# A two-layer hybrid decoder: the rotary table takes a buffer of the norms, and the last norm is cut differently between ScalarE, VectorE and GpSimd

## The chip, the cores and the metric

The kernel runs on one core of a Trainium2 chip. The metric is the device time of one execution in microseconds (us). A core has five engines: TensorE (PE in the profile, with its weight loads as PEld), VectorE (DVE), ScalarE (ACT), GpSimd (POOL) and SyncE (SP). Each works through its own list of instructions in order and waits on semaphores; all weights come in by DMAs that SP issues.

## The reference

One inference step of two decoder layers on 512 prompt tokens and 32 sample tokens (8 sequences of 4), width 1024, all float32. Cut to what matters here:

```python
def rms_norm(x, g):
    return x * lax.rsqrt(jnp.mean(x * x, axis=-1, keepdims=True) + NORM_EPS) * g

def partial_rope(x, pos):          # 16 of each head's 64 channels are rotated
    ang = pos[:, None] * inv[None, :]
    cos, sin = jnp.cos(ang), jnp.sin(ang)
    return jnp.concatenate([x1 * cos - x2 * sin, x2 * cos + x1 * sin, rest], -1)

def decoder_layer(x, start, st, prm):
    h = rms_norm(x, prm['g_mix_pre'])
    p_rw, p_s5, p_gdn, p_swa = split_cols(h @ prm['w_in'], PROJ_SPLITS)
    # RWKV-7 | S5 state space | gated DeltaNet | sliding-window attention (rotary on q and k)
    mix = jnp.concatenate([o_rw, o_s5, o_gdn, o_swa], -1) @ prm['w_out']
    x = x + rms_norm(mix, prm['g_mix_post'])
    h = rms_norm(x, prm['g_mlp_pre'])
    f = jnp.square(jax.nn.relu(h @ prm['w_up'])) @ prm['w_down']
    return x + rms_norm(f, prm['g_mlp_post'])
```

Outputs are the final x of all tokens and the updated states of the four mixers.

## The kernel before

The 544 tokens are columns and are worked on in two halves of 256 and 288 columns. Channels lie on the 128 partitions, eight tiles of 128 to the width. Activations of a half live in tiles named `acc` (128 x 8 x 288), the residual input is fetched back from DRAM as `xs`, `r` or `f`.

Every large product is made in three terms to keep float32 accuracy. A block of weights of 128 x 512 is loaded by SP (`wraw`, 256 KB, L1681, five buffers); ScalarE rounds it (`whi`, L232, three buffers); VectorE subtracts (`wlo`, L236, three buffers); TensorE then adds up hi x rh, hi x rl and lo x rh, twelve matmuls of 256 or 288 columns per block (L220), where rh and rl are the two parts of the activations (`h`, or `f` in the second half of the MLP). So each block needs one instruction of ScalarE, one of VectorE and one DMA, and a buffer of each of the three kinds comes free only when its readers are through.

A tile scheduler sets the order on each engine. It runs the program against its own model of time, with priorities for groups of work: mixers, norms, evacuations and weight loads. Code of one half is woven into the matrix products of the other in that way, so a changed buffer can move instructions far from the changed line. Buffers come from classes with a size and a count: `g2` (2304 bytes, 5 buffers) serves the mixers, `d2` (2304 bytes, 2 buffers) serves `prenorm`, `r2` and `r4` (5 buffers each) the mixers and the last norms. A tile of a class with no free buffer waits until the oldest one's last reader is done.

The order of the stages, each by layer and half: first projection, mixers of the first half beside the projection of the second, output product, MLP of one half beside the mixers of the other, and so on; the last stage is the second layer's MLP on the second half, with nothing left to weave in but the first half's final norm.

What the change and the prediction touch:

- `sw_begin` (L1085 to L1094) opens the sliding-window attention of a half. It takes a tile `rope` (cosines and sines, 128 x 2 x 288, so 256 to 288 KB), loads it with a DMA on SP (L1089) that is ordered after the last instruction of the gated DeltaNet before it, and `sw_evac` multiplies with it, once on GpSimd and once on VectorE for each of three tiles, when the projection of that half comes to the attention's columns. There are four such loads.
- `prenorm` (a few lines below `rms`) normalises a half ahead of a product. For each pair of tiles VectorE multiplies into a temporary of class `d2`, ScalarE scales two `h` tiles and VectorE makes the low parts, two instructions of the form SCALAR_TENSOR_TENSOR.
- `rms` and `rsqrt` (L1569 to L1582): two matmuls with a constant give the mean of squares, `preload_act_table_set` has ScalarE load a table (L1578, ACT_TABLE_LOAD) after the second matmul is placed, then come Ln and Exp on ScalarE. This happens 16 times in a run.
- `residual` (L1650 to L1672) computes x + norm. In the final one (`final`), it goes by four pairs of tiles, q = 0, 2, 4, 6: VectorE multiplies the pair by the norm, then adds the residual input; for q = 2 the addition is GpSimd's. SP writes each pair out (L1663). VectorE's order in the trace is four multiplies, then three additions.
- The final residual runs twice: for the first half inside the second half's MLP, for the second half as the end of the program.

Of the kernel before, what the change touches and what calls it, by code (L numbers as in the profile page):

```python
# [11 lines left out]
AF = mybir.ActivationFunctionType  # L12
ALU = mybir.AluOpType
# [6 lines left out]
HA = 288  # L20
# [119 lines left out]
class K:  # L140
# [944 lines left out]

    def sw_begin(self, l, half):
        n = HALVES[half][1]
        rope = self.w([128, 2, HA], "g2")[:, :, :n]
        d = self.nc.sync.dma_start(out=rope, in_=self.i["rope"][half, :, :, :n])  # L1089
        self.after(d, self.last_gd)  # L1090
        r = dict(n=n, half=half, x=self.place("sx", [128, 3, n]), v=self.place("sv", [128, n]), rope=rope)
        if half:
            r["prev"] = self.swprev
        return r  # L1094
# [471 lines left out]
        else:  # L1566
            self.last_sq = sq

    def rms(self, sums, sq):  # L1569

        n = sums.shape[1]
        mp = self.ps([128, n], "mn")
        self.mm(mp, self.mean.to_broadcast([128, 128]), sums, True, False)
        return self.rsqrt(sums, mp, self.mm(mp, self.mean.to_broadcast([128, 128]), sq, False, True))

    def rsqrt(self, out, mean, dep):

        t = self.nc.scalar.preload_act_table_set("natural_log_exp_and_others")  # L1578
        self.after(t, dep.ins)
        self.after(self.act(out, mean, AF.Ln, bias=self.eps), t.ins)  # L1580
        self.last_exp = self.act(out, out, AF.Exp, scale=-0.5)
        return out  # L1582

# [65 lines left out]
    def residual(self, half, src, sums, sq, cls, final=False):  # L1649


        c0, n = HALVES[half]
        xt = self.fetch(half, cls)
        rs = self.rms(sums, sq)
        step = 2 if final else 4
        new = None if final else self.row(half, "sums")
        mp = None
        for q in range(0, 8, step):
            a, xq = src[:, q:q + step], xt[q // 4][:, q % 4:q % 4 + step]
            self.tt(a, a, rs.unsqueeze(1).to_broadcast([128, step, n]))  # L1660
            self.tt(a, a, xq, ALU.add, eng=self.nc.gpsimd if final and q == 2 else None)
            if final:
                self.nc.sync.dma_start(out=self.o["yT"][:, q:q + step, c0:c0 + n], in_=a)  # L1663
            else:
                self.act(xq, a, AF.Square)
                mp = self.ps([128, n], "mn") if mp is None else mp
                for k in range(4):
                    m = self.mm(mp, self.mean.to_broadcast([128, 128]), xq[:, k], q + k == 0, q + k == 7)
        if final:
            return  # L1670
        self.x[half] = self.t([128, 8, n], f"x{half}", pool="dram", bufs=2)
        self.nc.gpsimd.dma_start(out=self.x[half], in_=src)  # L1672
        return self.rsqrt(new, mp, m)
# [387 lines left out]
```

## Time and profile before

| | |
|---|---|
| time, median of 3 runs | 1626.77 us (1626.5 to 1631.62) |
| profiled execution, its own time | 1630.86 us |
| its span, first to last instruction | 1629.1 us |
| PE busy in the span | 95% |
| PEld, DVE, ACT, POOL busy | 89%, 73%, 59%, 20% |
| mean granted clock of TensorE | 0.984 |
| DMA traffic | 267.38 MB, mean 164 GB/s |

The span and the rows below belong to the one profiled execution; it is 4.1 us above the median, inside what the three runs spread over. A name such as `wlo` stands for all buffers of that name; the line L236 is a helper that records every two-operand instruction, so what tells instructions apart there is what they read and write. A row that stands for several instructions gives the time from the first's start to the last's end.

### The profile page before, as it was taken

To read this page: it belongs to the slowest core of one execution; us is meant where nothing else is said; L and a number is where in the kernel's file an instruction comes from. 1 tells how busy PE (TensorE), PEld (TensorE's weight loads), DVE (VectorE), ACT (ScalarE), POOL (GpSimd) and SP (SyncE) were. 2 spreads that over 40 slices of the span, in tenths; PEclk is the share of its full clock that TensorE was granted. 3 is DMA by queue.
4 is the path that set the end of the run, shared out by engine and by line. 5 is a ranking of instruction groups with operands and counts; after the bars stand their busy time and mean duration, and the time that the engine had idled before them with its cause. 6 is when DMAs were issued, how large, how long until landed. Compare 5 with 4: busy or idle time off the path is not lost. (4 is left out here: it accounts for less than half of the span.)

```text
span 1629.1 us, 38773 instructions
## 1 busy us (share of the span) xinstructions
PE 1555.1 (95%) x14528; PEld 1453.4 (89%) x14528; DVE 1195.3 (73%) x2843; ACT 961.8 (59%) x2086; POOL 318.0 (20%) x618
## 2 busy tenths in 40 slices
PE   7989989899999999899999999999999999999996
PEld 7978978689889999888989999989888889999996
DVE  6898786976876867787595567879679755856665
ACT  6766648643455567765454467886444556755544
POOL 4751251000310428100020002620013001200001
PEclk9999999999999999999999999999999999999998
DMA  7645444443566565535365555535436655655552
GB/s 232 200 114 136 143 134 148 109 130 114 173 211 201 171 204 204 182 112 139 105 217 173 167 161 197 180 109 151 138 121 208 205 193 185 210 189 166 163 170 101
DMA packets 203112, 267.38 MB, mean 164 GB/s; under 512 B 81114, under 2 KB 95772, under 8 KB 202508
## 3 DMA queue, kind: packets, MB, share of 16 engines
q1 hardware_dynamic: 199180, 249.94, 48.9%
q0 software_dynamic: 3744, 14.96, 2.5%
q8 instruction: 114, 1.87, 0.5%
q14 instruction: 74, 0.61, 0.1%
HBM read 237.95 MB, written 28.58 MB: 164 GB/s over the span
## 5 line engine op out<-in xcount | busy, mean ns | idle before, releaser
L232 ACT CAST whi<-wraw 128x512 fp32r<-128x512 f32 x752 | 462.6, 619 | 419.2 <-PE ps L220 264.7
L236 DVE TENSOR_TENSOR wlo<-wraw,whi 128x512 fp32r<-128x512 f32 x752 | 534.9, 716 | 209.2 <-ACT whi L232 188.0
L220 PE MATMUL ps<-h,whi 128*128 128x288 f32 (+1 forms) x3264 | 519.5, 297 | 8.4 <-ACT h L228 4.4
L220 PEld LDWEIGHTS ps<-h,whi 128*128 128x128 f32 x3264 | 451.3, 191 | 25.8 <-ACT h L228 6.0
L220 PE MATMUL ps<-f,whi 128*128 128x288 f32 (+1 forms) x2752 | 421.9, 292 | 5.9 <-ACT whi L232 5.8
L220 PEld LDWEIGHTS ps<-f,whi 128*128 128x128 f32 x2752 | 372.0, 189 | 17.1 <-ACT whi L232 7.4
L220 PE MATMUL ps<-h,wlo 128*128 128x288 f32 (+1 forms) x1632 | 285.9, 295 | 5.4 <-DVE wlo L236 5.1
L220 PEld LDWEIGHTS ps<-h,wlo 128*128 128x128 f32 x1632 | 235.8, 191 | 12.3 <-DVE wlo L236 7.8
L220 PE MATMUL ps<-f,wlo 128*128 128x288 f32 (+1 forms) x1376 | 235.8, 292 | 1.7 <-DVE wlo L236 1.7
L220 PEld LDWEIGHTS ps<-f,wlo 128*128 128x128 f32 x1376 | 195.9, 189 | 5.3 <-DVE wlo L236 2.9
L236 POOL TENSOR_TENSOR sums<-sums,d 128x288 f32<-128x288 f32 (+1 forms) x54 | 51.2, 948 | 519.0 <-ACT d L228 517.7
L220 PE MATMUL ps<-r,r 64*64 64x64 f32 (+7 forms) x1184 | 67.8, 236 | 12.7 <-POOL r L236 3.8
L236 DVE TENSOR_TENSOR acc<-acc,ps 128x256 f32<-128x256 f32 (+1 forms) x96 | 41.7, 435 | 49.8 <-PE ps L220 49.7
L220 PEld LDWEIGHTS ps<-r,r 64*64 64x64 f32 (+4 forms) x1184 | 55.9, 140 | 23.2 <-issue 5.9
L232 ACT CAST f<-d 128x288 fp32r<-128x288 f32 (+1 forms) x128 | 53.3, 417 | 35.3 <-DVE d L236 35.3
L228 ACT ACTIVATE d<-ps 128x288 f32<-128x288 f32 (+1 forms) x152 | 59.8, 393 | 8.1 <-PE ps L220 6.1
L236 DVE TENSOR_TENSOR f<-d,f 128x288 fp32r<-128x288 f32 (+1 forms) x128 | 56.7, 443 | 7.4 <-ACT f L232 7.4
L236 DVE TENSOR_TENSOR d<-d 128x288 f32<-128x288 f32 (+1 forms) x128 | 56.7, 443 | 0.0
L228 ACT ACT_TABLE_LOAD x43 | 55.2, 1283 | 0.8
L220 PEld LDWEIGHTS ps<-t,t 64*64 64x64 f32 x1024 | 32.5, 135 | 4.7 <-issue 1.1
L220 PE MATMUL ps<-t,t 64*64 64x64 f32 x1024 | 36.3, 220 | 0.3 <-DMA t<-diag 0.2
L232 ACT COPY r<-ps 64x128 f32<-64x128 f32 (+2 forms) x56 | 20.4, 369 | 26.4 <-PE ps L625 11.6
(404 smaller groups left out, 1851.6 us busy)
## 6 DMA issues: line engine op xcount, KB each, us to landing
wraw<-in_w_up SPq DMA_DIRECT2D x256, 256.0 KB, 2.8
wraw<-in_w_down SPq DMA_DIRECT2D x256, 256.0 KB, 2.9
wraw<-in_w_in SPq DMA_DIRECT2D x176, 256.0 KB, 3.0
wraw<-in_w_out SPq DMA_DIRECT2D x64, 256.0 KB, 3.2
t<-diag SPq DMA_DIRECT2D x32, 128.0 KB, 3.2
x<-acc POOLq DMA_DIRECT2D x3, 1152.0 KB, 6.8
x<-acc POOLq DMA_DIRECT2D x3, 1024.0 KB, 6.4
xs<-mix SPq DMA_DIRECT2D x8, 288.0 KB, 2.9
```

Source lines behind the costliest of these rows:

```text
L220: return self.nc.tensor.matmul(out=out, lhsT=lhsT, rhs=rhs, start=start, stop=stop)
L228: return self.nc.scalar.activation(out=out, in_=in_, func=func, scale=scale, bias=bias, **kw)
L232: return self.nc.scalar.copy(out, in_)
L236: return (eng or self.nc.vector).tensor_tensor(out=out, in0=a, in1=b, op=op)
```

## The change

Three edits. The rotary table's tile is taken from `d2`, the two buffers of `prenorm`, instead of `g2`, the five of the mixers. `rms` and `rsqrt` get a flag, and the final residual of the second half asks for no ACT_TABLE_LOAD ahead of its Ln. In both final residuals, the pair q = 2 is multiplied on GpSimd as well as added there.

```diff
     def sw_begin(self, l, half):
         n = HALVES[half][1]
-        rope = self.w([128, 2, HA], "g2")[:, :, :n]
+        rope = self.w([128, 2, HA], "d2")[:, :, :n]
         d = self.nc.sync.dma_start(out=rope, in_=self.i["rope"][half, :, :, :n])
         self.after(d, self.last_gd)
...
-    def rsqrt(self, out, mean, dep):
-
-        t = self.nc.scalar.preload_act_table_set("natural_log_exp_and_others")
-        self.after(t, dep.ins)
-        self.after(self.act(out, mean, AF.Ln, bias=self.eps), t.ins)
+    def rsqrt(self, out, mean, dep, load=True):
+
+        ln = lambda: self.act(out, mean, AF.Ln, bias=self.eps)
+        if load:
+            t = self.nc.scalar.preload_act_table_set("natural_log_exp_and_others")
+            self.after(t, dep.ins)
+            self.after(ln(), t.ins)
+        else:
+            ln()
         self.last_exp = self.act(out, out, AF.Exp, scale=-0.5)
...
-        rs = self.rms(sums, sq)
+
+        rs = self.rms(sums, sq, not (final and half))
...
             a, xq = src[:, q:q + step], xt[q // 4][:, q % 4:q % 4 + step]
-            self.tt(a, a, rs.unsqueeze(1).to_broadcast([128, step, n]))
-            self.tt(a, a, xq, ALU.add, eng=self.nc.gpsimd if final and q == 2 else None)
+            eng = self.nc.gpsimd if final and q == 2 else None
+            self.tt(a, a, rs.unsqueeze(1).to_broadcast([128, step, n]), eng=eng)
+            self.tt(a, a, xq, ALU.add, eng=eng)
```

How the lists of instructions move, with the numbers of the buffers as the scheduler gave them. On SP, the rotary load of the second layer's first half stands 83 places later, between the weight blocks that were issued at 619.91 and 621.94 us in the trace of before, and waits there for a `d2` buffer; the second layer's other one stands three weight blocks later. The two of the first layer keep their places.

On DVE, the `prenorm` ahead of the first layer's MLP on the second half, which starts at 648.84 us in the trace of before: `d_2144` to `d_2147` are the four products in `d2` buffers, `h_2143` the low parts made from them, `xs_9094` work of the second layer's RWKV mixer.

```order
 L236 TENSOR_TENSOR wlo_9421<-wraw_9419,whi_9420 128x512
 L245 SCALAR_TENSOR_TENSOR h_2143_11270<-d_2144_11271,pf_73,h_2142_11269 128x288
+L236 TENSOR_TENSOR wlo_9452<-wraw_9450,whi_9451 128x512
+L236 TENSOR_TENSOR d_2145_11277<-acc_8396,sums_8788 128x576
+L245 SCALAR_TENSOR_TENSOR xs_9094<-e_1787_9394,pf_75,xs_9094 128x256
+L236 TENSOR_TENSOR wlo_9470<-wraw_9468,whi_9469 128x512
 L245 SCALAR_TENSOR_TENSOR h_2143_11270<-d_2145_11277,pf_73,h_2142_11269 128x288 x2
-L236 TENSOR_TENSOR wlo_9452<-wraw_9450,whi_9451 128x512
+L236 TENSOR_TENSOR wlo_9497<-wraw_9495,whi_9496 128x512
 L236 TENSOR_TENSOR d_2146_11283<-acc_8396,sums_8788 128x576
-L245 SCALAR_TENSOR_TENSOR xs_9094<-e_1787_9394,pf_75,xs_9094 128x256
-L236 TENSOR_TENSOR d_2147_11289<-acc_8396,sums_8788 128x576
```

In the order before, the multiply of `d_2145` stood right behind that of `d_2144`, ahead of these rows. It now follows the readers of `d_2144`; that of `d_2146` follows the readers of `d_2145`, and that of `d_2147` stands further on.

On PE, the products of that MLP (`ps_12065`, `ps_12107`, `ps_12149`, units of `w_up`) around the first S5 product (`ps_11078`), whose operand `r_2101` GpSimd makes; in the trace of before this is the stretch from 833 to 843 us.

```order
-L220 MATMUL ps_12107<-h_2142_11269,whi_12109 128x288 x4
+L220 MATMUL ps_12107<-h_2142_11269,whi_12109 128x288
+L220 MATMUL ps_12065<-h_2142_11269,wlo_12086 128x288 x4
+L220 MATMUL ps_12107<-h_2142_11269,whi_12109 128x288 x3
 L220 MATMUL ps_12107<-h_2143_11270,whi_12109 128x288 x4
+L220 MATMUL ps_12107<-h_2142_11269,wlo_12110 128x288 x4
+L220 MATMUL ps_12107<-h_2142_11269,whi_12127 128x288 x4
 L220 MATMUL ps_11078<-r_2101_11054,r_2106_11071 64x64 x2
 L220 MATMUL ps_11107<-r_2101_11054,r_2106_11071 64x64 x2
-L220 MATMUL ps_12065<-h_2142_11269,wlo_12086 128x288 x4
-L220 MATMUL ps_12149<-h_2142_11269,whi_12151 128x288 x4
-L220 MATMUL ps_12149<-h_2143_11270,whi_12151 128x288 x4
```

Twelve more matmuls of the MLP (`wlo_12086`, `wlo_12110`, `whi_12127`) now stand ahead of the S5 product, whose matmuls keep their own order.

On DVE, the final residual of the first half, from 1417.45 us in the trace of before: `acc_17066` is that half, `sums_17067` its norm, `r_3820` and `r_3821` the residual input; `f`, `d` and `wlo` belong to the second half's MLP.

```order
-L236 TENSOR_TENSOR acc_17066<-acc_17066,sums_17067 128x2x256 x4
+L236 TENSOR_TENSOR acc_17066<-acc_17066,sums_17067 128x2x256 x3
 L236 TENSOR_TENSOR wlo_20220<-wraw_20218,whi_20219 128x512
 L236 TENSOR_TENSOR acc_17066<-acc_17066,r_3820_20111 128x2x256
 L236 TENSOR_TENSOR f_3811_20068<-d_3819_20106,f_3810_20067 128x288
 L236 TENSOR_TENSOR d_3830_20170<-d_3830_20170 128x288
-L236 TENSOR_TENSOR acc_17066<-acc_17066,r_3821_20112 128x2x256
+L236 TENSOR_TENSOR acc_17066<-acc_17066,r_3821_20112 128x2x256 x2
 L236 TENSOR_TENSOR wlo_20238<-wraw_20236,whi_20237 128x512
-L236 TENSOR_TENSOR acc_17066<-acc_17066,r_3821_20112 128x2x256
```

One multiply is gone from the run of four ahead of `wlo_20220`, and two additions instead of one stand ahead of `wlo_20238`; on GpSimd a multiply stands ahead of the addition, and on SP the four writes of this half stand in a row instead of between weight blocks.

In the last residual there are now three multiplies and three additions on DVE, a multiply and an addition on POOL, and on ACT Ln right behind its work for the mean. Of SP's four writes there, GpSimd's pair was first before and is second now, behind the pair q = 0.

## Rows read from the trace of the kernel before

**Rows 1.** the page, part 1: engine, busy us, share of the span, instructions

```profile
PE 1555.1 (95%) x14528; PEld 1453.4 (89%) x14528; DVE 1195.3 (73%) x2843; ACT 961.8 (59%) x2086; POOL 318.0 (20%) x618
```

**Rows 2.** last MLP: us, busy us of PE, PEld, DVE, ACT, POOL, clock

```profile
1410.00:1616.00 206.00, 205.75 (x1543) 204.85 (x1542) 127.32 (x227) 111.16 (x219) 7.59 (x8) 1.00 0.51 165
```

**Rows 3.** what PE waited for: total us, times, longest us

```profile
PE ps L220 <- DVE wlo L236: 6.8, 12, 1.7
```

**Rows 4.** timeline of the tail: start, us, engine, line, operation, [idle before]

```profile
1616.56 0.75 PE L220 MATMUL ps<-e,mean 128*128 128x288 f32 x2 [0.53 <-ACT e L228]
1617.10 1.28 ACT L1578 ACT_TABLE_LOAD   x1
1618.39 0.50 ACT L228 ACTIVATE sums<-ps,eps 128x288 f32<-128x288 f32 x1
...
1619.40 3.96 DVE L236 TENSOR_TENSOR acc<-acc,sums 128x576 f32<-128x576 f32 x4 [3.36 <-ACT sums L228]
1620.90 1.85 POOL L236 TENSOR_TENSOR acc<-acc,xs 128x576 f32<-128x576 f32 x1 [6.55 <-DVE acc L236]
...
1623.29 2.08 DVE L236 TENSOR_TENSOR acc<-acc,xs 128x576 f32<-128x576 f32 x3
```

**Rows 5.** timeline, a norm between layers, PE and ACT

```profile
627.07 0.65 PE L220 MATMUL ps<-e,mean 128*128 128x288 f32 x2
...
627.82 0.50 ACT L228 ACTIVATE sums<-ps,eps 128x288 f32<-128x288 f32 x1 [0.24 <-POOL s5v L242]
```

**Rows 6.** timeline, final residual of the first half, inside the last MLP

```profile
1417.45 3.59 DVE L236 TENSOR_TENSOR acc<-acc,sums 128x512 f32<-128x512 f32 x4
...
1418.82 1.67 POOL L236 TENSOR_TENSOR acc<-acc,r 128x512 f32<-128x512 f32 x1 [5.91 <-DVE acc L236]
...
1420.96 0.68 DVE L236 TENSOR_TENSOR wlo<-wraw,whi 128x512 fp32r<-128x512 f32 x1
...
1422.08 0.70 PE L220 MATMUL ps<-h,wlo 128*128 128x288 f32 x4
...
1423.51 0.68 DVE L236 TENSOR_TENSOR wlo<-wraw,whi 128x512 fp32r<-128x512 f32 x1
...
1424.75 0.69 PE L220 MATMUL ps<-h,wlo 128*128 128x288 f32 x4
```

**Rows 7.** timeline around 621 us, DVE and SP

```profile
620.42 0.87 DVE L245 SCALAR_TENSOR_TENSOR f<-d,pf,f 128x256 fp32r<-128x256 f32 x2
...
621.94 0.93 SPq L1681 DMA_DIRECT2D wraw<-in_w_in  x2
```

**Rows 8.** DMA, 619 to 632 us: GB/s in 40 slices; issues, KB, landing

```profile
GB/s 214 44 0 0 0 38 221 397 170 6 0 13 145 347 303 189 258 171 100 136 182 234 248 298 362 379 390 393 395 405 401 457 377 381 382 389 398 391 384 328
...
wraw<-in_w_in SPq DMA_DIRECT2D x8, 256.0 KB, 7.3
```

**Rows 9.** timeline, PE after those loads

```profile
632.93 1.22 PE L220 MATMUL ps<-f,whi 128*128 128x256 f32 x8 [0.27 <-ACT whi L232]
634.60 1.21 PE L220 MATMUL ps<-f,whi 128*128 128x256 f32 x8 [0.46 <-ACT whi L232]
```

**Rows 10.** timeline, low parts of the moved norm, and their first reader

```profile
658.96 1.80 DVE L245 SCALAR_TENSOR_TENSOR h<-d,pf,h 128x288 fp32r<-128x288 f32 x4
...
722.03 0.83 PE L220 MATMUL ps<-h,whi 128*128 128x288 f32 x5
```

**Rows 11.** timeline, PE's larger gaps from 648 to 840 us

```profile
657.22 0.50 PE L220 MATMUL ps<-f,whi 128*128 128x256 f32 x2 [2.90 <-ACT whi L232]
...
663.99 1.21 PE L220 MATMUL ps<-f,whi 128*128 128x256 f32 x8 [0.85 <-ACT whi L232]
...
702.99 0.70 PE L220 MATMUL ps<-e,cst 128*128 128x256 f32 x2 [1.11 <-ACT e L232]
...
708.48 1.16 PE L220 MATMUL ps<-r,r 64*128 64x128 f32 x16 [0.82 <-DVE r L236]
...
837.18 0.45 PE L220 MATMUL ps<-r,r 64*64 64x64 f32 x8 [2.08 <-POOL r L236]
```

More of the change, by code (lines that the diff above doesn't have):

```diff
@@ L1567, in square_sum, with rms @@
             self.last_sq = sq
-    def rms(self, sums, sq):
+    def rms(self, sums, sq, load=True):
         n = sums.shape[1]
@@ L1573, in rms @@
         self.mm(mp, self.mean.to_broadcast([128, 128]), sums, True, False)
-        return self.rsqrt(sums, mp, self.mm(mp, self.mean.to_broadcast([128, 128]), sq, False, True))
-    def rsqrt(self, out, mean, dep):
-        t = self.nc.scalar.preload_act_table_set("natural_log_exp_and_others")
-        self.after(t, dep.ins)
-        self.after(self.act(out, mean, AF.Ln, bias=self.eps), t.ins)
+        return self.rsqrt(sums, mp, self.mm(mp, self.mean.to_broadcast([128, 128]), sq, False, True), load)
+    def rsqrt(self, out, mean, dep, load=True):
[6 more added lines that the diff above has]
+            ln()
         self.last_exp = self.act(out, out, AF.Exp, scale=-0.5)
```

## The prediction

> **What bounds the kernel now.** I read the page's busy shares first: TensorE is busy for 1555.1 us of the span [rows 1], so a change moves the time in two places only, where TensorE waits and where it has ended. Then the busy time by stretches: in the last MLP TensorE is busy for 205.75 of 206 us, and VectorE for 127.32 [rows 2], so VectorE's work counts there only if a `wlo` comes late. TensorE's list of waits holds such cases, 12 of them with 6.8 us together and 1.7 us at the longest [rows 3]. Last I read the timeline of the tail, where nothing hides anything [rows 4].
>
> **The last table load.** The two matmuls of the mean end at 1616.56 + 0.75 = 1617.31, ACT_TABLE_LOAD runs from 1617.10 to 1618.38 and Ln starts at 1618.39 [rows 4]. Without the load Ln waits for TensorE alone. The row nearest to that is the norm at 627, where ScalarE had loaded earlier: the matmuls end at 627.72 and Ln starts at 627.82, 0.10 later [rows 5]. So Ln starts at 1617.41 and the tail gains 0.98 us. Bounds: 0 if ScalarE finds something else to wait for, 1.08 if Ln follows TensorE at once. The load shows no idle time ahead of it, and Ln follows 0.01 us behind it [rows 4]. The Trainium skill (ScalarE: Activation LUTs, What ACT_TABLE_LOAD costs) puts a switch to another set at about 2.66 us, 1.283 of load and 1.380 of drain. The load agrees with the row's 1.28; a drain would bring the gain to some 2.4 us, an estimate from that page, but the rows leave it no room on either side, and I give it no chance.
>
> **GpSimd's multiply in the tail.** Three VectorE additions take 2.08 us, 0.69 each, with GpSimd idle; the four multiplies take 3.96 where 4 x 0.69 = 2.77 would do, with GpSimd's 1.85 us inside their time [rows 4]. So GpSimd's one operation takes 1.19 us out of VectorE's, and the two do not run side by side. Before: 3.96 + 2.08, less the overlap of 0.07, is 5.97 from 1619.40 to 1625.37. After: six VectorE operations, 6 x 0.69 = 4.16, and two of GpSimd at 1.19, 2.38, together 6.54. That is 0.57 longer. Bounds: if the second GpSimd operation costs VectorE nothing, one multiply less, -0.69; if both shut VectorE out for their full 1.85, 4.16 + 3.70 = 7.86, +1.9. I take +0.57, since it uses the only rate that the rows show for this pair of shapes. SP's last write stays that of a VectorE pair, behind the last addition, so what follows it stays. Tail: -0.98 + 0.57 = **-0.4** us, between -1.8 and +1.9.
>
> **The same multiply in the first half's residual.** It lies inside the last MLP. Four multiplies of 512 columns took 3.59 us [rows 6]; at 0.69 x 512/576 = 0.62 each they would take 2.47, so GpSimd's 1.67 us cost VectorE 1.12 here. After the change: 3 x 0.62 + 2 x 1.12 = 4.10, which is 0.51 longer. Behind that stands a `wlo` that ended at 1421.64 and that TensorE took at 1422.08: 0.44 us of slack, so it comes 0.07 late. The next one ended at 1424.19 and was taken at 1424.75, 0.56 of slack [rows 6]; it has the 0.51 and one more addition of 0.62 ahead of it, and comes 0.57 late. TensorE loses the larger of the two, and the loss stays, since this stretch has no idle time in which to make it up: **+0.6** us. Bounds: 0 if GpSimd's multiply slips behind the first `wlo`; if both operations block in full, 1.86 + 3.34 = 5.20, which is 1.61 longer, and the second `wlo` comes 1.61 + 0.62 - 0.56 = 1.7 late. SP issues four writes in a row there before its next weight block; that block is for later, and its other buffers cover it.
>
> **The rotary load.** The loads of the first layer and the second layer's last one stay in or near their places; I cost them at nothing, and lose nothing if wrong, as their readers come tens of us later. The second layer's first one moves into a crowd. Its wait for a `d2` buffer costs nothing: the buffer's last readers end at 620.42 + 0.87 = 621.29, and the weight load behind it was issued at 621.94 [rows 7], so SP is not held and neither are the weights queued behind. But 256 KB more then lie ahead of the loads that take 7.3 us to land, in slices that move some 390 GB/s [rows 8]; 0.262 MB at that rate is 0.67 us. TensorE then already waits 0.27 and 0.46 us for the `whi` made from them [rows 9], so there is no cover left and I count it in full: **+0.7** us, between 0 (the casts wait for a free buffer) and 1.0 (several blocks late).
>
> **The buffer that is gone.** With the table in one of two `d2` buffers, the four multiplies of the norm for the first layer's second MLP go one at a time. The low parts ended at 658.96 + 1.80 = 660.76, and TensorE first reads the result at 722.03 [rows 10]; even 10 us later nobody waits for it. The other norm of this kind, for the second layer's first half, is cheap for the same reason. What it does cost or give is order: from there to 840 us the scheduler weaves VectorE's and TensorE's lists anew. Five of TensorE's waits there sum to 7.76 us [rows 11]. In the new order twelve more matmuls stand ahead of the S5 product that waited 2.08 us for GpSimd; at 1.21/8 = 0.15 us each [rows 9] they cover up to 1.8. Two stand ahead of the product that waited 1.11 (0.5 covered, with their loads), and eleven ahead of the one that waited 0.82 (all of it). Of the 2.90 us at 657.22 about 1.0 goes, as TensorE takes the blocks that are there first; but ScalarE then comes later to the block at 663.99, whose wait grows by about 0.75. Together -1.8 - 0.5 - 0.8 - 1.0 + 0.75 = -3.35. A new order also brings waits at places that had none, and no trace of before shows them, while I looked for gains only where a wait stood. I keep half: **-1.7** us, between -3.4 and +3.4, the same on the other side.
>
> **Sum.** -0.4 + 0.6 + 0.7 - 1.7 = -0.8 us. Against the profiled execution's own 1630.86 this gives 1630.1. That execution lies 4.1 us above the median, with a span shorter by 1.8; the terms are differences, so on the median they give 1626.77 - 0.8 = **1626.0**. A difference of 0.3%, 4.9 us, is about what a measurement of this kernel can tell from none.
>
> **The rivals.** (a) The new order closes the waits without opening others: all of the 3.35, then as much again from the mixers beyond 1000 us, whose lists on TensorE also move, with the tail and the residual at their good ends (-0.4 and 0) and the load hidden: -7, so 1619.8. For it: 7.76 us of waits lie there. Against it: waits are there because operands are late, and matmuls put ahead only help if their own weights are ready. (b) GpSimd and VectorE shut one another out in full, and the load is late: tail +0.9 (-0.98 + 1.9), residual +1.7, load +1.0, order 0, together +3.6, so 1630.4. For it: GpSimd's 1.85 us cost VectorE 1.19 already. The Trainium skill (GPSIMD Engine Reference, 4.1 Engine selection) gives element-wise work with two inputs to VectorE, GpSimd being about 2 times slower; that speaks against this edit, and the rows, 1.85 against 0.69 us with both at work, show a wider ratio. (c) Slower: the norm that now goes through one `d2` buffer stalls VectorE. Each of its last three multiplies stands behind ScalarE's reading of the pair before it, and `wlo` blocks stand behind the multiply in VectorE's list. If ScalarE is held by a late weight block, TensorE waits for those `wlo` too; with one wait like the 2.90 of [rows 11] at two of the three, and the load's 0.7, +6.5 and 1633.3. It decides once ScalarE's copies come later than VectorE has other work, some 0.7 us by one instruction. (d) The change does not do what it says: Ln is held until 1618.39 by another wait, so the 0.98 is lost: +0.2, 1627.0. Against it: no load is left in ScalarE's list there.
>
> **How the numbers follow.** The forecast has 0.50, (a) 0.18, (b) 0.12, (c) 0.12, (d) 0.08. Faster by over 0.3% is (a), 0.18; slower is (c), 0.12; the others, 0.70, are no change. The range leaves out the far half of (a) and of (c), some 2 in 10 with the tails of the rest: from 1620.5 to 1631.
>
> **What would show it.** In the trace after: Ln 0.1 us behind the mean's matmuls, with no load; six VectorE and two GpSimd operations over about 6.5 us in the tail; TensorE waits of about half a us near 1424; landings of the weight blocks near 630 later by 0.7; the wait at 837 mostly gone. The forecast is wrong if the tail shrinks by over 1 us, if VectorE waits for ScalarE around 650, or if TensorE's waits after 1000 change by more than 3 us.

## The result: slower by 0.67%

| | before | changed |
|---|---|---|
| median | 1631.43 us (6 runs, 1626.5 to 1635.82) | 1643.43 us (6 runs, 1639.01 to 1646.34) |
| profiled execution, time and span | 1630.86, 1629.1 us | 1644.34, 1642.6 us |

The ratio is 1.0067, with a 95% interval of 1.0045 to 1.0089: some 11 us slower, where the prediction had 0.8 us faster and a range up to 1631.0. The median of before rose with three more runs, from 1626.77 to 1631.43, so an unchanged time would lie just past that range as well; what counts is the difference between the two kernels. The same program spreads over 10 us and more from one execution to the next, which matters below.

The page of the changed kernel, parts 1 and 2, which answers to [rows 1]:

```profile
span 1642.6 us, 38775 instructions
...
PE 1565.0 (95%) x14528; PEld 1460.0 (89%) x14528; DVE 1198.9 (73%) x2841; ACT 961.0 (59%) x2085; POOL 321.8 (20%) x620
```

TensorE does the same 14528 matmuls and is busy for 9.9 us longer, out of 13.5 us of span. So most of the loss is no waiting: the matmuls themselves took longer. The mean granted clock says the same for a part of it, 0.981 after 0.984.

To see where, I laid the two traces side by side by ScalarE's 752 casts of weight blocks (`whi`), which come in the same number and nearly the same order in every kernel here. The time between two such casts is a stretch that holds the same work. Later traces of the experiments are in the same table. Lost clock is one minus the granted clock, summed over the stretch; waits are TensorE's gaps over 0.1 us, and the rest is what is left of the stretch without either.

| blocks | about, us | rotary table in g2, 5 traces | rotary table in d2, 5 traces |
|---|---|---|---|
| 0 to 240 | 7 to 604 | 596.4 to 600.7 | 594.2 to 601.9 |
| 240 to 340 | 604 to 849 | 244.6 to 247.9 | 246.1 to 247.9 |
| 340 to 512 | 849 to 1182 | 332.7 to 333.5 | 332.8 to 334.2 |
| 512 to 600 | 1182 to 1366 | 179.5 to 183.5 | 187.6 to 189.4 |
| its lost clock | | 1.7 to 3.4 | 5.1 to 6.8 |
| its waits | | 2.9 to 5.3 | 4.8 to 5.8 |
| its rest | | 174.5 to 174.8 | 176.7 to 177.0 |
| 600 to 744, GpSimd as before or without | 1366 to 1599 | 233.3 to 233.6 | 233.3 to 233.4 |
| 600 to 744, GpSimd multiplies | 1366 to 1599 | 235.2 | 234.7 to 235.2 |

(The five on the left are before, before again, the residual edits alone and two kernels without GpSimd in the residuals; on the right the changed kernel three times, the table alone, and one load of the table alone.) One stretch stands out, 1182 to 1366 us, for which the prediction's sum had no term. It takes 188.6 us in the mean on the right and 181.1 on the left. The first 604 us differ by several us among traces of one program, so the 4.5 us by which the first trace of the changed kernel was late at 75 us are nothing of the change.

### The profile page after: what moved, and what is told of

It reads as the page before. It is cut to its first block, busy times and chain, and to the rows that moved or that the text cites. A ratio compares the mean times of both kernels' runs of the same rounds, so it can differ in the third digit from the quotient of the medians.

```text
span 1642.6 us, 38775 instructions
## 1 busy us (share of the span) xinstructions
PE 1565.0 (95%) x14528; PEld 1460.0 (89%) x14528; DVE 1198.9 (73%) x2841; ACT 961.0 (59%) x2085; POOL 321.8 (20%) x620
## 5 line engine op out<-in xcount | busy, mean ns | idle before, releaser
L232 ACT COPY r<-ps 64x128 f32<-64x128 f32 (+2 forms) x56 | 20.4, 369 | 28.7 <-PE ps L625 11.2
```

Of the source, the lines that this page charges most:

```text
L232: return self.nc.scalar.copy(out, in_)
```

## What TensorE does in the stretch that lost

TensorE in the kernel before, from 1223 to 1236 us; the columns are start, us, engine, line, operation, operands, tile, count.

```profile
1223.45 1.97 PE L220 MATMUL ps<-cst,gdlb 32*128 32x32 f32 x16
1225.35 0.75 PE L220 MATMUL ps<-r,cst 128*128 128x288 f32 x2
...
1227.48 0.63 PE L220 MATMUL ps<-h,wlo 128*128 128x256 f32 x4
1227.95 1.10 PE L220 MATMUL ps<-h,whi 128*128 128x256 f32 x8
...
1230.89 2.04 PE L220 MATMUL ps<-cv,s 64*64 64x8 f32 x64
1232.86 0.75 PE L220 MATMUL ps<-xs,rwg 128*128 128x288 f32 x2
```

And in the changed kernel, the same work:

```profile
1235.09 1.97 PE L220 MATMUL ps<-cst,gdlb 32*128 32x32 f32 x16
1236.98 1.33 PE L220 MATMUL ps<-cv,s 64*64 64x8 f32 x40
1238.25 0.75 PE L220 MATMUL ps<-r,cst 128*128 128x288 f32 x2
1238.93 0.51 PE L220 MATMUL ps<-cv,s 64*64 64x8 f32 x10
1239.37 0.90 PE L220 MATMUL ps<-xs,rwg 128*128 128x288 f32 x2
1240.21 1.02 PE L220 MATMUL ps<-cv,s 64*64 64x8 f32 x14
1241.16 0.79 PE L220 MATMUL ps<-h,whi 128*128 128x256 f32 x2
1241.75 1.05 PE L220 MATMUL ps<-h,wlo 128*128 128x256 f32 x4
```

`gdlb` and `cv,s` are the gated DeltaNet's products with the eight sample states, on 32 by 128 and 64 by 64 pieces of the array. Before, five and a half us of dense matmuls (128 by 128 pieces) lie between them; now 40 of the 64 `cv,s` products follow `gdlb` at once, and the other 24 come between four dense matmuls. The busy time around the `cv,s` products of before, and of the microseconds behind `gdlb` in the changed kernel (the columns after the length are PE, PEld, DVE, ACT, POOL with counts, granted clock, DMA share, GB/s):

```profile
1228.00:1232.00 4.00, 4.00 (x59) 3.51 (x60) 3.33 (x8) 2.34 (x5) 1.74 (x4) 1.00 0.37 126
1232.00:1236.00 4.00, 4.00 (x65) 3.58 (x64) 3.74 (x14) 1.03 (x3) 0.17 (x1) 1.00 0.42 143
```

```profile
1236.00:1240.00 4.00, 4.00 (x64) 3.20 (x63) 3.49 (x10) 1.02 (x3) 0.97 (x2) 0.98 0.39 118
1240.00:1244.00 4.00, 4.00 (x26) 3.48 (x26) 1.26 (x3) 0.62 (x1) 0.00 (x0) 0.50 0.00 0
1244.00:1248.00 4.00, 4.00 (x23) 3.71 (x21) 2.18 (x7) 1.00 (x2) 0.36 (x2) 0.67 0.21 70
```

From 1240 us the clock is at 0.50, 1.2 GHz in place of 2.4, and four dense matmuls (`h,wlo`) take 1.05 us, where four of the same kind take 0.63 in the rows of before. TensorE is busy for all of the 4.00 us ahead of the fall, mostly with small products. At 1228 to 1236 us, around the same products of before, the clock is 1.00. The Trainium skill (TensorE: Matmul & The Clock Gate, Why this matters for your kernels) ties drops in the middle of a kernel to gaps in which TensorE idles; here there is no gap, so the trace shows a case beside that one.

## The experiments

All figures are against the kernel before on the same chip, with 23 to 32 runs of it beside each set. Each run also gives its granted clock, so (1 - clock) x time is the clock's loss of that run. Means over the runs, us:

| kernel | runs | time - before | clock's loss - before | ratio, 95% interval |
|---|---|---|---|---|
| rotary table alone (e1) | 7 | +6.9 | +3.9 | 1.0043, 1.0027 to 1.0059 |
| residual edits alone (e2) | 12 | +0.6 | -1.7 | 1.0002, 0.9988 to 1.0015 |
| changed kernel (e3) | 6 | +8.9 | +4.6 | 1.0054, 1.0034 to 1.0074 |
| before (e4) | 12 | -0.8 | -0.6 | 0.9996, 0.9976 to 1.0016 |
| small products apart (e5) | 12 | +6.1 | +1.6 | 1.0036, 1.0017 to 1.0054 |
| before, small products joined (e6) | 12 | +2.3 | +2.1 | 1.0011, 0.9996 to 1.0025 |
| one load of the table alone (e7) | 9 | +7.7 | +5.0 | 1.0053, 1.0032 to 1.0074 |
| no load, no GpSimd (e8) | 12 | -1.5 | -0.7 | 0.9992, 0.9977 to 1.0007 |
| the same by pairs (e9) | 12 | -1.3 | -1.5 | 0.9993, 0.9980 to 1.0006 |
| small products apart (e10) | 12 | +3.7 | -0.6 | 1.0019, 1.0004 to 1.0034 |
| changed kernel (e11) | 6 | +9.4 | +4.0 | 1.0057, 1.0037 to 1.0077 |

**Which edit.** The kernel before with the table's line alone (e1), and with the two residual edits without it (e2):

```diff
-        rope = self.w([128, 2, HA], "g2")[:, :, :n]
+        rope = self.w([128, 2, HA], "d2")[:, :, :n]
```

```diff
-        rs = self.rms(sums, sq)
+        rs = self.rms(sums, sq, not (final and half))
...
-            self.tt(a, a, rs.unsqueeze(1).to_broadcast([128, step, n]))
-            self.tt(a, a, xq, ALU.add, eng=self.nc.gpsimd if final and q == 2 else None)
+            eng = self.nc.gpsimd if final and q == 2 else None
+            self.tt(a, a, rs.unsqueeze(1).to_broadcast([128, step, n]), eng=eng)
+            self.tt(a, a, xq, ALU.add, eng=eng)
```

> The kernel before with the first edit alone: the rotary table's tile from d2. The lists of all engines are those of the changed kernel up to the first half's final residual. Theory A (the loss is the new weave from 648 us on and the late rotary load): 8 to 10 us slower than before, ratio 1.005 to 1.006, with the steps of the shift at 510 to 520, 640 to 700 and 1235 to 1247 us in the trace as in the changed kernel. Theory B (the loss is made by GpSimd's multiplies and the tail): within 2 us of before.

> The kernel before with the second and third edit: no table load ahead of the last Ln, GpSimd multiplies one pair in both final residuals; the rotary table stays in g2. All lists are those of before up to 1417 us. Theory A: 0 to 2 us slower (the tail was 0.44 us longer in the trace of the changed kernel and TensorE waited some 1 us more around 1420), ratio 1.000 to 1.001. Theory B: 8 to 12 us slower.

The table's buffer makes seven of the nine us, a little under the 8 to 10 of theory A. The residual edits are not to be told from zero by the times of their runs, though their trace shows 1.7 to 1.8 us in the last MLP and 0.4 in the tail; without the clock's loss, which was 1.7 us lower in those runs, they stand 2.3 us above before. Theory B falls. But not all of theory A stands: the loss is not spread over the weave from 648 us on, it lies at 1182 to 1366.

**What is chance.** The changed kernel and the kernel before, once more.

> The changed kernel once more. Its first 630 us have the same lists as before, yet its trace was 4.5 us late by 75 us and 6.1 late by 530. Theory A: this spread is of the execution, not of the program, so the shift at 75 us comes out differently here, by some us, while the shift between 640 and 1400 stays at 5 to 8 us; time 9 to 13 us above before. Theory C (holding one d2 buffer from the start already slows the first stage, with no change of order): the shift at 75 us is again 4 to 5 us.

> The kernel before, as one of the kernels, for the spread of traces and of times. Theory A: ratio 1.000 within 0.002; its trace differs from the other trace of before by up to 5 us at 75 us and the number of stretches at the lower granted clock (12 ahead of the tail) differs by one or two. Theory C: the shift at 75 us is within 1 us of the first trace.

At 75 us the second trace of the changed kernel was 0.8 us ahead of the first trace of before, where the first was 4.5 behind. Theory C, which I had thought of only on seeing that 4.5, is gone: holding a `d2` buffer from the start costs nothing in the first stage, and its lists are those of before. The rest is near what theory A gave: 8.9 us above before, and a shift that grows by 7.4 us between 640 and 1400 us. At 500 us the two traces of before differ by 3.5 us and those two of the changed kernel by 5.8, of which lost clock makes 1.0 and 3.4.

**Which load.** Only the second layer's first half takes its table from d2.

```diff
-        rope = self.w([128, 2, HA], "g2")[:, :, :n]
+        rope = self.w([128, 2, HA], "d2" if (l, half) == (1, 0) else "g2")[:, :, :n]
```

> The kernel before with the table of the second layer's first half alone in d2, the other three in g2. Theory A (one load decides the new weave): as with all four, ratio 1.0035 to 1.0055, the stretch from block 512 to 600 at 187 to 189 us. Rival (the second half's table, which holds a d2 buffer during the norm at 1033 us, makes it): ratio within 0.002 of 1, the stretch below 184 us.

It has the whole loss of the table, 189.4 us in the stretch, a little over what theory A gave, and a ratio inside its range. One buffer that is taken from 621 to 708 us changes what stands side by side on TensorE 500 us later.

**The small products.** An order, and no wait on data, puts the `cv,s` products behind the RWKV norm's last product again, in the changed kernel:

```diff
-            self.mm(bp, self.c("ones64"), q)
+            self.rwbp = self.mm(bp, self.c("ones64"), q).ins
...
-                    self.mm(sp[rs, p, b], s0[rs, p, b], kq[rs, :, :, b])
+                    m = self.mm(sp[rs, p, b], s0[rs, p, b], kq[rs, :, :, b])
+                    if l and p + b + hh == 0:
+                        self.after(m, self.rwbp)
```

> The changed kernel, with one order added in the second layer: the 64 products with the gated DeltaNet's sample states (cv,s) come behind the last product of the RWKV norm, as they do in the list of before, so eight dense matmuls stand between the gdlb products and them. Everything ahead of that point keeps the changed kernel's lists. In three traces with the rotary table in d2 the stretch from weight block 512 to 600 (about 1182 to 1366 us) took 187.6 to 188.8 us, in three without it 179.5 to 183.5. Theory P (TensorE loses there because small products, gdlb and cv,s, stand back to back: the granted clock falls for 3.4 us or twice that, and changes of tile shape come more often): the stretch comes back to 180 to 184 us, the ratio to before to 1.001 to 1.003. Theory Q (the loss is spread over the new weave, or comes from waits): the stretch stays at 187 to 189, the ratio at 1.005.

TensorE in the second set of this kernel, e10:

```profile
1236.05 1.97 PE L220 MATMUL ps<-cst,gdlb 32*128 32x32 f32 x16
...
1239.73 1.12 PE L220 MATMUL ps<-h,whi 128*128 128x256 f32 x8
...
1242.20 2.04 PE L220 MATMUL ps<-cv,s 64*64 64x8 f32 x64
```

```profile
1240.00:1244.00 4.00, 4.00 (x80) 3.62 (x78) 3.75 (x11) 1.39 (x4) 0.52 (x2) 1.00 0.34 117
```

The 64 products take 2.04 us again, as before, and the clock stays at 1.00. The stretch came to 181.9 us in e5 and 184.2 in e10; its rest, without lost clock and waits, is 174.9 and 174.8, near the kernels with the table in g2. The ratio of e5, 1.0036, was above what theory P gave and below that of theory Q; that of e10, 1.0019, was inside P's. The set e10 is the direct comparison, beside the changed kernel:

> The changed kernel with the small products apart, once more, on the same chip as the next one, for a direct comparison. Theory P: 2 to 5 us below the changed kernel's mean, the clock's loss (one minus the granted clock, times the span) lower by 2 to 4 us, the stretch from block 512 to 600 at 180 to 184 us. Theory Q: within 1.5 us of the changed kernel.

> The changed kernel, for the comparison with the one before this. Theory P: ratio to before 1.005 to 1.007, the stretch from block 512 to 600 at 187 to 189 us with the lower clock next to the gdlb and cv,s products. Theory Q: the lower clock lies elsewhere in this execution.

5.7 us less in the mean, 4.6 of them clock, a little more than theory P gave. This places most of the loss. Of the 3.7 us that stay, the residual edits account for 1.5 to 2 by the traces.

The order added does not undo the rest of 2.1 us where it arises, though. From block 512 to 532 of TensorE's own list (up to about 1250 us), with nearly the same matmuls in all of them, the rest is 56.3 us with the table in g2, 57.8 to 58.0 in d2, and 58.1 to 58.3 with the small products apart. The last get as much back at blocks 556 to 588 (1290 to 1354 us), where their list came out in another order: 55.1 us for the same matmuls that take 56.9 to 57.1 in the ten traces of the table of stretches.

The converse, in the kernel before, with the `rwbp` line as above:

```diff
-            self.mm(bp[:, h, 0], lb[:NS, 2, 4 + h:5 + h].to_broadcast([NS, 128]), self.c("tris")[:NS])
+            m = self.mm(bp[:, h, 0], lb[:NS, 2, 4 + h:5 + h].to_broadcast([NS, 128]), self.c("tris")[:NS])
+            if l and h == 0:
+                self.after(m, self.rwbp)
```

> The converse: the kernel before, with the gdlb products of the second layer ordered behind the last product of the RWKV norm, so that they stand right ahead of the cv,s products; all lists are those of before up to there. Theory P: the stretch from block 512 to 600 grows from 179.5 to 183.5 us to 185 to 189 and the granted clock falls next to the two groups; ratio 1.002 to 1.004. Theory Q: the stretch stays below 184 us, ratio within 0.0015 of 1.

TensorE there, and the clock around it:

```profile
1237.88 1.97 PE L220 MATMUL ps<-cst,gdlb 32*128 32x32 f32 x16
1239.78 3.20 PE L220 MATMUL ps<-cv,s 64*64 64x8 f32 x64
```

```profile
1236.00:1240.00 4.00, 4.00 (x37) 3.47 (x35) 4.00 (x12) 1.64 (x4) 2.51 (x4) 1.00 0.37 125
1240.00:1244.00 4.00, 4.00 (x66) 3.39 (x62) 0.89 (x3) 0.00 (x0) 0.00 (x0) 0.54 0.14 48
1244.00:1248.00 4.00, 4.00 (x33) 3.69 (x32) 2.83 (x11) 0.81 (x2) 0.68 (x3) 0.61 0.20 76
```

Put together in a kernel without any of the three edits, the two groups bring the clock down at the same spot, and `cv,s` takes 3.20 us. In the six traces in which they stand together (five with the table in d2, and this one) the clock falls between 1231 and 1241 us, each time while the `cv,s` products are under way, at a loss of 3.4 us in five and 1.7 in one; in the seven others it falls nowhere between 1211 and 1259 us. The stretch is 185.2 us, at the low end of what theory P gave, and its rest is 174.5, as without the table in d2. The ratio, 1.0011, is below what theory P gave and inside theory Q's range; the time, +2.3 us, has an interval that still holds zero, and it is less than the edit's seven: lost clock is a part of the loss, not all.

**The residuals.** No last table load, and VectorE does all eight operations (e8, the edits of e2 with `eng = None`); then the same with the last residual pair by pair (e9):

```diff
-            self.tt(a, a, rs.unsqueeze(1).to_broadcast([128, step, n]))
-            self.tt(a, a, xq, ALU.add, eng=eng)
+            m = self.tt(a, a, rs.unsqueeze(1).to_broadcast([128, step, n]))
+            if final and half and q:
+                self.after(m, add.ins)
+            add = self.tt(a, a, xq, ALU.add)
```

> The kernel before without the last table load and with GpSimd taken out of both final residuals, so VectorE does all eight operations; the rotary table stays in g2. Theory E (a GpSimd operation takes 1.2 us out of VectorE's time, an own one 0.69): from the start of the mean's last matmuls to the end of the span 10.8 to 11.4 us in place of 12.54 (0.98 from the load, about 0.45 from VectorE), and the stretch from block 600 to 744 at 232.8 to 233.6 us in place of 233.5 before and 235.0 with the change; ratio 0.998 to 1.000. Rival (the two engines work side by side): the tail no shorter than 11.9 us.

> The kernel before without the last table load, with VectorE doing both final residuals, and in the last one pair by pair: multiply, add, write, then the next pair. Theory W (the tail of the changed kernel grew because four writes stand in a row behind the first addition, 4.6 us from the last addition to the end of the span against 3.7 before): the writes spread, the last addition stays at the same distance, 10.4 to 11.1 us from the mean's last matmuls to the end of the span (11.22 with four multiplies first); ratio 0.997 to 1.000. Rival (the end is set by the last write alone): 11.2 us as before.

The tail of e8, which answers to [rows 4]:

```profile
1615.38 0.75 PE L220 MATMUL ps<-e,mean 128*128 128x288 f32 x2 [0.54 <-ACT e L228]
1616.23 0.50 ACT L228 ACTIVATE sums<-ps,eps 128x288 f32<-128x288 f32 x1 [0.34 <-PE ps L220]
...
1617.24 2.76 DVE L236 TENSOR_TENSOR acc<-acc,sums 128x576 f32<-128x576 f32 x4 [2.39 <-ACT sums L228]
1619.92 2.76 DVE L236 TENSOR_TENSOR acc<-acc,xs 128x576 f32<-128x576 f32 x4
1620.70 2.41 SPq L1669 DMA_DIRECT2D out_yT<-acc  x4
```

Eight operations on VectorE alone take 5.44 us, less than seven with GpSimd's one among them, 5.97 [rows 4], or six with two, 6.50. The tail, from the mean's last matmuls to the end of the span, is 11.2 us, against 12.5 before, as theory E gave; the stretch from block 600 to 744 is 233.4, as before. By pairs the tail stays at 11.2, so theory W is wrong: the writes no longer stand in a row and the last one lands 2.2 us after its issue in place of 2.7, but each addition now waits for its own multiply, and the last ends 0.5 us later. Both kernels lie below the kernel before in the mean, by 1.5 and 1.3 us, which their intervals don't tell from zero.

## The prediction, step by step

**The table load** held: Ln starts 0.10 us behind the matmuls of the mean, as forecast. The tail of the changed kernel:

```profile
1629.62 0.75 PE L220 MATMUL ps<-e,mean 128*128 128x288 f32 x2 [0.54 <-ACT e L228]
1630.47 0.50 ACT L228 ACTIVATE sums<-ps,eps 128x288 f32<-128x288 f32 x1 [0.34 <-PE ps L220]
...
1631.48 4.50 DVE L236 TENSOR_TENSOR acc<-acc,sums 128x576 f32<-128x576 f32 x3 [2.39 <-ACT sums L228]
1631.52 1.97 POOL L236 TENSOR_TENSOR acc<-acc,sums 128x576 f32<-128x576 f32 x1 [4.12 <-ACT sums L228]
1633.57 1.79 POOL L236 TENSOR_TENSOR acc<-acc,xs 128x576 f32<-128x576 f32 x1
1635.90 2.08 DVE L236 TENSOR_TENSOR acc<-acc,xs 128x576 f32<-128x576 f32 x3
1636.67 2.12 SPq L1669 DMA_DIRECT2D out_yT<-acc  x4
```

**GpSimd's multiply in the tail** held: VectorE needs 6.50 us, from 1631.48 to 1637.98, where I had 6.54. **What follows it** did not. I wrote that SP's last write stays and so what follows it stays. The last addition is indeed 0.44 us earlier, counted from the mean's matmuls (8.36 against 8.80), yet the end of the span is 0.4 later. GpSimd's pair was ready first before, and its write went out ahead of the others; now it stands behind the pair q = 0, four writes go within 2.12 us, and the last lands 3.23 us after its issue, against 2.55. That is 0.7 us for the landing and 0.2 for the queue on SP, and both edits of the tail are lost in it: +0.4 us, where the sum had -0.4. The new order of the writes was known, from the lists; its cost was put at nothing.

**The first half's residual** was too small: +0.6 predicted, +1.1 to +1.9 in four traces (234.7 to 235.2 against 233.3 to 233.6). On TensorE's list the first `wlo` that I named costs 0.2 us, the second brings the delay to 0.75, and a third one, 7.5 us behind it, to 0.9 to 1.3. I had taken the larger of the first two for the whole. What lies above 1.3 is not the residual's: it is a wait of 0.6 and 0.8 us for a `whi` at 1412 and 1424 us, ahead of GpSimd's multiply, in two of the four traces.

**The rotary load** costs nothing that can be told: TensorE's waits behind it were 0.27 and 0.46 us [rows 9] and are 0.3 to 1.6 and 0.46 to 0.47 in the traces with the table in d2, but three traces without it have a wait of 2.0 to 2.6 us at a neighbouring block. The fourth weight load there lands after 7.7 to 8.9 us in d2 and 6.7 to 8.3 without, so it does come later, but the 0.7 can't be told in TensorE's waits.

**The buffer that is gone** is the step that failed, and with it the sentence that the prediction starts from, that a change moves the time in two places only, where TensorE waits and where it has ended. The local part had the right sign in four waits of five. PE's gaps in the changed kernel, which answer to [rows 11]:

```profile
660.41 1.21 PE L220 MATMUL ps<-f,whi 128*128 128x256 f32 x8 [1.44 <-ACT whi L232]
...
669.83 2.14 PE L220 MATMUL ps<-f,whi 128*128 128x256 f32 x16 [0.75 <-ACT whi L232]
...
694.07 0.68 PE L220 MATMUL ps<-cst,c 128*128 128x130 f32 x4 [1.53 <-DVE c L242]
...
708.27 2.05 PE L220 MATMUL ps<-c,cst 128*128 128x256 f32 x4 [3.37 <-DVE g L242]
...
847.40 2.55 PE L220 MATMUL ps<-r,r 64*64 64x64 f32 x80 [1.01 <-POOL r L236]
```

2.90 became 1.44, 2.08 became 1.01 (where up to 1.8 was to be covered), 1.11 and 0.82 are gone, and the 0.85 did not grow; new waits of 3.37 and 1.53 us took it back, as the text feared. The stretch from 604 to 849 us is 0.3 us longer in the mean, not 1.7 shorter. What failed is that the term ended at 840 and priced waits alone.

The order of the two programs also differs at 1200 to 1260 us, and I put that under rival (a), as more of the same waits to be gained. There the loss is mostly no wait: of 7.4 us in the stretch (means of 188.55 and 181.13), 3.8 are lost clock, 3.1 of them at `gdlb` and `cv,s`, 1.5 waits over 0.1 us, and 2.1 the rest. With +0.4 in the tail and some +1.2 at the residual that makes 9.0 us, as the means of e3 and e11 have it, 8.9 and 9.4. The rest is nearly the same in each of the five traces. It goes with the number of times that TensorE passes from one tile shape to another between blocks 512 and 600: 78 in e6 and 79 with the table in g2 (174.5 to 174.8 us), 83 in e5 and e10 (174.8 and 174.9), 90 in d2 (176.7 to 177.0). That such changes are its cause was not tested by a run. The text named a change of over 3 us in TensorE's waits after 1000 us as a sign that would make it wrong; they went from 7.4 to 9.4 us in the traces with g2 to 9.0 to 10.4 in those with d2, and matmuls that take longer were not among its signs. Rival (c), the norm that stalls VectorE, had the right sign and a wrong place: near 660 us VectorE waits 2.1 to 3.2 us for one `whi` in the traces with the table in d2, but 0.6 to 3.6 in those without it, and TensorE's wait there is the shorter one in d2 (1.2 to 1.8 us against 2.0 to 2.9).

What stays open: the 2.1 us of the rest were not laid to single instructions, and the 1.5 us of waits in that stretch stay in e5 and e10, so they have another cause in the new order. The joined groups cost 2.3 us in the kernel before, nearly all of it clock, and the split gives 5.7 in the changed one beside it (2.8 by e5 and e3, which ran on two chips); a part of that is the other order at 1290 to 1354 us, so its clock, 4.6 us, is the safer figure for the two groups. In e1, e6, e10 and e11 the clock also fell once at 1205 to 1207 us, behind the 64 products `c,s` that all kernels have there.

## What to carry to other kernels

A buffer's class is an input to the scheduler: read the whole of the two lists, to the end, and price a place where the order differs even if nothing waits there. On an engine that is 95% busy, look for what makes its instructions longer, here groups of small products put side by side, not for its gaps alone. When work moves to another engine, follow what was queued behind it as far as the last DMA.

## What the runs showed of the hardware

The granted clock fell to 0.50 with TensorE busy without a gap, in the course of 64 products on 64 by 64 pieces with 8 columns that stood behind 16 on 32 by 128, in six traces of six in which these stand together, and stayed at 1.00 there in the seven traces with 4.2 to 5.5 us of dense matmuls between them. Executions of one program spread over up to 16 us in this kernel (1623.8 to 1639.9 in e4), along with 20 to 39 us of lost clock. A GpSimd operation on 128 x 576 elements took 1.8 to 2.0 us and cost VectorE 1.2 us [rows 4]. Four writes of 288 KB that are issued within 2.12 us land in 3.23 us for the last; when they are 1.5 us apart (e9), it takes 2.2.
